# A float32 decoder trunk on one Trainium2 core: the split weights moved by 12 bytes modulo 512, the recurrent section's split operands moved along, the norm's spread written as transposes

## The chip, the core and the metric

The kernel runs on one core of a Trainium2 chip. The metric is the device time of one execution in microseconds. The engines are named as in the profile: PE is TensorE's matmul, PEld its weight load, DVE VectorE, ACT ScalarE, POOL GpSimd, SP the engine that issues most of the DMAs.

## The reference

Two layers over 256 tokens of width 1024 in float32, each a token mixer and a squared-ReLU MLP of width 4096, with RMS norms before each and at the end. Layer 0 mixes with a gated recurrence (RG-LRU), layer 1 with sparse attention.

```python
for i in range(DEPTH):                       # 2 layers
    h = _rmsnorm(x, norm_mix[i])
    if i % N_MIXERS == 0:
        x = x + _rglru_mixer(h, rg_w_in, conv, rg_w_a, rg_w_x, rg_lambda, rg_w_out)
    else:
        x = x + _nsa_mixer(h, nsa_w_in, ..., nsa_w_out)
    h = _rmsnorm(x, norm_ffn[i])
    x = x + _sq_relu_mlp(h, mlp_w_up[i], mlp_w_down[i])    # relu(h @ up)^2 @ down
return _rmsnorm(x, norm_final)

def _rmsnorm(x, g):
    return x * rsqrt(mean(x * x, -1) + 1e-6) * g
```

The inputs are x (1, 256, 1024) and the weights, the output has the shape of x, all in float32.

## The kernel before

Everything is held transposed: a tile `xt` of 128 partitions by 8 chunks by 256 tokens holds x. A linear layer multiplies a piece of weights (128 rows by 128 columns, the stationary operand, loaded by PEld) with 256 tokens of activations (the moving operand). To keep float32's precision with TensorE's faster format (float32r), each operand is split into a high part and the remainder, and one product takes three matmuls (`mm3`): high weights with high activations (line 313), high weights with low activations (314), low weights with high activations (315). This form makes up nearly all the matmuls:

```python
    def mm3(ps, wh, wl, xh, xl, start, stop):
        pe.matmul(ps, wh, xh, start=start, stop=False)
        pe.matmul(ps, wh, xl, start=False, stop=False)
        pe.matmul(ps, wl, xh, start=False, stop=stop)
```

Weights come as pieces of 128 x 1024 floats through five raw buffers (`raw`). ACT (or DVE) rounds a piece into one of seven buffers `whi` (lines 273 and 321), DVE subtracts to get `wlo` (lines 282 and 318). A piece is 8 weight blocks of 128 columns, 512 bytes a partition each, and serves 24 matmuls.

The moving operands are: `hhl`, the normed activations with high and low part, for every input projection and the MLP's up-projection; `uhl`, the MLP's hidden activations, for the down-projection; `xbh` and `xbl`, the split result of the recurrence, for its out-projection; `oh` and `ol` for attention's. The gates of the recurrence multiply unsplit float32 weights `gw` with `xb` (line 656).

A norm sums squares over partitions with matmuls against ones (line 491), takes the root and the reciprocal per token as a column `rcol`, and `spread` (line 494 on) turns that column back into a row on all partitions: a matmul with `rcol` broadcast along 128 columns against the identity (line 496), twice, once for each 128 tokens. It is called once in the recurrent section, once at the start of each MLP, once in the attention section and once for the final norm.

In the recurrent and attention sections a planner with costs and due times orders the instructions; in the MLPs the order is as written. The tile pools place the tiles in the order in which they are asked for. Pool `weights` holds the `whi` and `wlo` tiles one behind the other, then come the statistics, then the section's own tiles; the raw buffers, `hhl` and `uhl` are placed from the other end. So the place of a tile is fixed when the program is built. Start addresses in bytes along a partition, modulo 512:

| tile | before | after the change |
|---|---|---|
| whi, wlo (all blocks) | 32 | 20 |
| hhl, uhl, oh, ol, raw | 480 | 480 |
| xbh, xbl | 352 | 480 |
| xb, r, i, y, t | 352 | 352 |
| gw, a2 | 448 | 64 |
| xp (three) | 352, 384, 416 | 480, 0, 32 |

The rest of the tiles keep their place modulo 512.

Of the kernel before, what the change touches and what calls it, by code (L numbers as in the profile page):

```python
# [12 lines left out]
F32 = mybir.dt.float32  # L13
F32R = mybir.dt.float32r
# [5 lines left out]
P = 128  # L20
S = 256
# [9 lines left out]
NRAW, NSPL = 5, 7  # L31
# [193 lines left out]
def trunk_kernel(ctx: ExitStack, tc: tile.TileContext, x_in, vec_in, const_in, w2_in, wts, out):  # L225
    nc = tc.nc
    ctx.enter_context(tc.manual_schedule())
    pe, dve, act, pool = nc.tensor, nc.vector, nc.scalar, nc.gpsimd
# [5 lines left out]
    wpool = ctx.enter_context(tc.tile_pool(name="weights", bufs=1))  # L234
# [3 lines left out]
    def bank(i):  # L238
        return psum.tile([P, 512], F32, name="bank%d" % i, tag="bank%d" % i)
# [9 lines left out]
    WMAX = 1024  # L249
    LOOK = 6  # L250
    raw_t = [rpool.tile([P, WMAX], F32, name="raw%d" % i) for i in range(NRAW)]
    hi_t = [wpool.tile([P, WMAX], F32R, name="whi%d" % i) for i in range(NSPL)]
    lo_t = [wpool.tile([P, WMAX], F32R, name="wlo%d" % i) for i in range(NSPL)]

    def load(i, parts=1):
        n = piece_cols(*order[i])
# [71 lines left out]
    class Section:  # L328
# [73 lines left out]
        def stats(self, srcs, t):  # L402

            b6 = [("ps", 6)]
            st = self.bank(("stats", t), 6, lambda x: x)
            for j, (x, k) in enumerate(srcs):
                self.add("pe", 0.32, lambda e, j=j, x=x: square_sums(st(), x, j == 0, j == len(srcs) - 1), r=[k], w=b6, t=t)
            self.add("act", 0.15, lambda e: e.activation(rcol, st()[:, :2], AF.Sqrt, bias=epst, scale=1.0 / D), r=b6 + ["tab"],
                     w=["rcol"], t=t)
            self.add("dve", 0.08, lambda e: e.reciprocal(rcol, rcol), w=["rcol"], t=t)  # L410
            self.add("pe", 0.43, lambda e: spread(st()), r=["rcol", "cst"], w=b6, t=t)
            self.add("act", 0.26, lambda e: e.copy(rs, st()[:, S:]), r=b6, w=["rs"], t=t)
# [36 lines left out]
    ident = cst[:, C_ID:C_ID + P]  # L449
# [7 lines left out]
    rcol = spool.tile([P, 2], F32, name="rcol")  # L457
# [35 lines left out]
    def spread(st):  # L493

        for i in range(2):
            pe.matmul(st[:, S + i * P:S + (i + 1) * P], rcol[:, i:i + 1].to_broadcast([P, P]), ident, start=True, stop=True)

    def residual(z, m):
        dve.tensor_tensor(xt[:, m], xt[:, m], z, op=OP.add)  # L499
# [2 lines left out]
    with ExitStack() as ph:  # L502
        rg = ph.enter_context(tc.tile_pool(name="rg", bufs=1))
# [91 lines left out]
        small(lambda e: e.tensor_scalar(sp, sp, 4.0, None, op0=OP.mult), [], ["sp"])  # L595

        xb_b, r_b, i_b, y_b, t_b = (rg.tile([P, 8, S], F32, name=n) for n in ("xb", "r", "i", "y", "t"))
        xbh_b, xbl_b = (rg.tile([P, 8, S], F32R, name=n) for n in ("xbh", "xbl"))
        xb, r_t, i_t, y_t, t_t, xbh, xbl = ([x[:, m] for m in range(8)] for x in (xb_b, r_b, i_b, y_b, t_b, xbh_b, xbl_b))
        pair = lambda x, m: x[:, m // 2 * 2:m // 2 * 2 + 2]  # L600
# [665 lines left out]
    st = bank(6)  # L1266
    mlp(1, to_final, up1, lambda: square_sums(st, acc, True, False))
    square_sums(st, sqs[1], False, True)
    act.activation(rcol, st[:, :2], AF.Sqrt, bias=epst, scale=1.0 / D)
    dve.reciprocal(rcol, rcol)  # L1270
    spread(st)

    for i, (a, n) in enumerate(((0, 1), (1, 1), (2, 2), (4, 2), (6, 1), (7, 1))):
# [113 lines left out]
```

## Time and profile before

| | |
|---|---|
| device time, median of 3 runs | 593.89 us (592.77 to 594.01) |
| span of the profiled execution, first to last instruction | 588.7 us |
| what lies between that span and the median | 5.2 us |
| instructions | 12309 |
| mean granted TensorE clock | 0.996 |
| matmul records / weight loads | 4798 / 4798 |

The profiled execution gives its span alone; its own device time is not listed beside it, so a time worked out on the span is carried to the median by those 5.2 us. Times in the profile's rows are counted from the first instruction. A matmul's record has a start and a modelled end, and the next one starts before that end; how fast PE runs is read from the distance of starts. A group's row gives line, engine, operation, output and inputs by tile names, shapes, count, then busy time, mean ns of one, and idle time ahead of it with what ended it.

In order of time the span holds the recurrent section (to about 93 us), the first MLP (to about 270), attention (to about 410) and the second MLP with the final norm.

### The profile page before, as it was taken

What the parts mean: (1) busy time and instruction counts of PE and PEld (TensorE: products, weight loads), DVE (VectorE), ACT (ScalarE), POOL (GpSimd) and SP (SyncE); (2) the same over time, 40 slices, a digit from 0 to 9 for tenths busy, and PEclk for the clock granted to TensorE, in tenths of its full rate; (3) what the DMA queues carried; (4) which work ended last, traced back from release to release, by engine and by line L of the source; (5) the groups of instructions that cost most, each with busy time, mean ns of one, the idle gap of its engine ahead of it and who ended that gap; (6) DMA issues with size and microseconds to landing.
All of it is one profiled execution on the core that took longest, in us unless ns stands there. A gap on an engine that the chain in (4) does not pass through costs nothing.

```text
span 588.7 us, 12309 instructions
## 1 busy us (share of the span) xinstructions
PE 572.6 (97%) x4798; PEld 559.1 (95%) x4798; DVE 421.5 (72%) x862; ACT 356.5 (61%) x711; POOL 75.2 (13%) x110
## 2 busy tenths in 40 slices
PE   7999999999999999999999999989999999999994
PEld 7999999999999999999989997879999999999994
DVE  6899997776766546547679999989876776464522
ACT  7699583766664325336367999996866564343410
POOL 2210000000001113125211532000000000132320
PEclk9999999999999999999999999999999999999998
DMA  8934665665666665657954641143776667466302
GB/s 285 386 119 136 208 221 183 216 206 183 192 201 197 210 205 175 210 188 228 232 197 144 180 128 52 37 125 99 238 201 199 188 206 239 158 183 228 126 2 72
DMA packets 32682, 105.74 MB, mean 180 GB/s; under 512 B 4832, under 2 KB 6496, under 8 KB 32624
## 3 DMA queue, kind: packets, MB, share of 16 engines
q1 hardware_dynamic: 30224, 100.70, 53.3%
q0 software_dynamic: 1824, 3.72, 2.5%
q8 instruction: 38, 0.62, 0.5%
q10 hardware_dynamic: 576, 0.53, 0.3%
q14 instruction: 20, 0.16, 0.1%
HBM read 99.23 MB, written 1.05 MB: 170 GB/s over the span
## 4 chain that ended last, share of the span: by engine, by line
PE 81%; ACT 8%; DVE 6%; issue 3%; DMA 1%; POOL 0%; SPq 0%; DVEq 0%; ACTq 0%; POOLq 0%
PE bank L315 25%; PE bank L313 25%; PE bank L314 25%; PE bank L656 2%; ACT pt L1105 2%; ACT pt L1124 2%; DVE wlo L318 1%; ACT pth L1138 1%; ACT whi L321 1%; PE bank L906 1%; DMA raw<-in_dram 1%; ACT osum L1171 1%; DVE ptl L1139 1%; DVE pt L1102 1%; DVE osum L1174 1%
## 5 line engine op out<-in xcount | busy, mean ns | idle before, releaser
L313 PE MATMUL bank<-hhl,whi 128*128 128x256 f32 x768 | 214.3, 279 | 1.6 <-DVE whi L321 1.6
L315 PE MATMUL bank<-hhl,wlo 128*128 128x256 f32 x768 | 212.7, 277 | 0.8 <-DVE wlo L318 0.8
L314 PE MATMUL bank<-hhl,whi 128*128 128x256 f32 x768 | 212.3, 276 | 0.0
L282 DVE TENSOR_TENSOR wlo<-raw,whi 128x1024 fp32r<-128x1024 f32 x118 | 147.3, 1269 | 2.7 <-ACT whi L273 2.7
L313 PEld LDWEIGHTS bank<-hhl,whi 128*128 128x128 f32 x768 | 144.2, 188 | 2.2 <-ACT whi L321 1.5
L315 PEld LDWEIGHTS bank<-hhl,wlo 128*128 128x128 f32 x768 | 144.2, 188 | 1.6 <-DVE wlo L318 1.4
L314 PEld LDWEIGHTS bank<-hhl,whi 128*128 128x128 f32 x768 | 144.4, 188 | 0.1
L313 PE MATMUL bank<-uhl,whi 128*128 128x256 f32 x512 | 141.4, 276 | 0.0
L315 PE MATMUL bank<-uhl,wlo 128*128 128x256 f32 x512 | 141.4, 276 | 0.0
L314 PE MATMUL bank<-uhl,whi 128*128 128x256 f32 x512 | 141.4, 276 | 0.0
L273 ACT CAST whi<-raw 128x1024 fp32r<-128x1024 f32 x119 | 120.9, 1039 | 23.7 <-issue 18.8
L314 PEld LDWEIGHTS bank<-uhl,whi 128*128 128x128 f32 x512 | 96.1, 188 | 0.0
L313 PEld LDWEIGHTS bank<-uhl,whi 128*128 128x128 f32 x512 | 96.1, 188 | 0.0
L315 PEld LDWEIGHTS bank<-uhl,wlo 128*128 128x128 f32 x512 | 96.1, 188 | 0.0
L318 DVE TENSOR_TENSOR wlo<-raw,whi 128x1024 fp32r<-128x1024 f32 (+3 forms) x72 | 76.0, 1073 | 2.6 <-ACT whi L321 2.6
L499 DVE TENSOR_TENSOR xt<-xt,bank 128x256 f32<-128x256 f32 x40 | 16.0, 417 | 85.6 <-PE bank L315 85.4
L321 ACT CAST whi<-raw 128x1024 fp32r<-128x1024 f32 (+2 forms) x65 | 61.5, 957 | 17.4 <-PE bank L314 9.5
L751 ACT ACTIVATE u<-t 128x256 f32<-128x256 f32 x64 | 26.7, 417 | 54.9 <-DVE t L746 54.9
L746 DVE SCALAR_TENSOR_TENSOR t<-bank,rstd 128x256 f32<-128x256 f32 x64 | 26.9, 423 | 42.5 <-PE bank L315 41.7
L469 POOL TENSOR_TENSOR acc<-xt 128x256 f32<-128x256 f32 x2 | 3.0, 1522 | 301.1 <-DVE xt L499 301.1
L1264 ACT ACTIVATE xg<-xt,vec 128x256 f32<-128x256 f32 x8 | 4.1, 510 | 48.0 <-DVE xt L499 48.0
L1105 ACT ACTIVATE pt<-pt,mx 128x256 f32<-128x256 f32 (+1 forms) x64 | 28.7, 452 | 3.4 <-DVE mx L1102 3.2
(201 smaller groups left out, 830.5 us busy)
## 6 DMA issues: line engine op xcount, KB each, us to landing
raw<-in_dram SPq DMA_DIRECT2D x175, 512.0 KB, 4.3
gw<-in_dram SPq DMA_DIRECT2D x4, 512.0 KB, 8.4
raw<-in_dram SPq DMA_DIRECT2D x6, 256.0 KB, 5.3
xt<-in_dram SPq DMA_DIRECT2D x4, 256.0 KB, 5.0
kh<-th POOLq DMA_DIRECT2D x16, 64.0 KB, 4.2
raw<-in_dram SPq DMA_DIRECT2D x2, 456.0 KB, 4.8
zwoh<-in_dram SPq DMA_DIRECT2D x1, 512.0 KB, 4.9
zwol<-in_dram SPq DMA_DIRECT2D x1, 512.0 KB, 6.2
```

Source lines behind the costliest of these rows:

```text
L273: (act.copy if eng is None else eng.tensor_copy)(hi_t[i % NSPL][:, :n], raw_t[i % NRAW][:, :n])
L282: (eng or dve).tensor_tensor(lo[:, :n], raw_t[i % NRAW][:, :n], hi[:, :n].bitcast(F32), op=OP.subtract)
L313: pe.matmul(ps, wh, xh, start=start, stop=False)
L314: pe.matmul(ps, wh, xl, start=False, stop=False)
L315: pe.matmul(ps, wl, xh, start=False, stop=stop)
L318: return lambda e: e.tensor_tensor(o, a, h.bitcast(F32), op=OP.subtract)
L321: return lambda e: (e.copy if e is act else e.tensor_copy)(o, a)
L499: dve.tensor_tensor(xt[:, m], xt[:, m], z, op=OP.add)
L656: e.matmul(z(), gw[b][:, o:o + P], xb[2 * b + k], start=k == 0, stop=k == 1)
L746: dve.scalar_tensor_tensor(t, z, 0.0, rs, op0=OP.max, op1=OP.mult)
L751: act.activation(u, t, AF.Square)
L1105: add("act", (0.39, 0.49)[qc], lambda e, row=row, j=j: e.activation(row, row, AF.Exp, bias=mx[:, j:j + 1], scale=-1.0, accum_out=sm[:, j:j ...
```

## The change

The fourteen tiles of split weights become slices of one tile `whl`, each 1024 floats; 120 floats are left free ahead of it and the slices begin 5 floats into it. So all weights lie 12 bytes lower modulo 512, and what follows them in memory lies 512 bytes higher, the same modulo 512. In the recurrent section 32 floats are left free ahead of `xbh` and `xbl`, which moves these two and what follows them (`xp`, `a2`, `gw`) by 128 bytes: `xbh` and `xbl` stand at the same distance from the weights as `hhl` does. The two matmuls of `spread` become transposes (a matmul with the transpose flag) of the same operands. Every engine executes the same instructions in the same order with the same waits.

```diff
     raw_t = [rpool.tile([P, WMAX], F32, name="raw%d" % i) for i in range(NRAW)]
-    hi_t = [wpool.tile([P, WMAX], F32R, name="whi%d" % i) for i in range(NSPL)]
-    lo_t = [wpool.tile([P, WMAX], F32R, name="wlo%d" % i) for i in range(NSPL)]
+    wpool.tile([P, 120], F32, name="wgap")
+    w_all = wpool.tile([P, 2 * NSPL * WMAX + 8], F32R, name="whl")
+    hi_t, lo_t = ([w_all[:, 5 + (i + j * NSPL) * WMAX:5 + (i + j * NSPL + 1) * WMAX] for i in range(NSPL)] for j in range(2))
 
@@
     def spread(st):
 
         for i in range(2):
-            pe.matmul(st[:, S + i * P:S + (i + 1) * P], rcol[:, i:i + 1].to_broadcast([P, P]), ident, start=True, stop=True)
+            pe.transpose(st[:, S + i * P:S + (i + 1) * P], rcol[:, i:i + 1].to_broadcast([P, P]), ident)
 
@@
         xb_b, r_b, i_b, y_b, t_b = (rg.tile([P, 8, S], F32, name=n) for n in ("xb", "r", "i", "y", "t"))
+        rg.tile([P, 32], F32, name="rgap")
         xbh_b, xbl_b = (rg.tile([P, 8, S], F32R, name=n) for n in ("xbh", "xbl"))
```

## The prediction

> **What bounds the kernel now.** I read the shares of the engines first, then the chain that ended last, then the busy time of the engines in stretches of 20 us, and last the starts of single matmuls. Page, engines' shares and the chain by engine and line:
>
> ```profile
> PE 572.6 (97%) x4798; PEld 559.1 (95%) x4798; DVE 421.5 (72%) x862; ACT 356.5 (61%) x711; POOL 75.2 (13%) x110
> PEclk9999999999999999999999999999999999999998
> PE 81%; ACT 8%; DVE 6%; issue 3%; DMA 1%; POOL 0%; SPq 0%; DVEq 0%; ACTq 0%; POOLq 0%
> ```
>
> TensorE (PE) is the bound: 97% busy, 81% of the chain, at the full granted clock. "Busy" hides how fast it runs, since matmuls overlap. The stretches (each: width, then busy time and instructions of PE, PEld, DVE, ACT, POOL, then clock and DMA) say where nothing else holds it:
>
> ```profile
> 0.00:20.00 20.00, 16.70 (x125) 15.92 (x126) 14.16 (x35) 13.98 (x31) 5.44 (x12) 1.00 0.86 308
> 40.00:60.00 20.00, 20.00 (x160) 19.48 (x159) 20.00 (x32) 19.82 (x33) 0.00 (x0) 1.00 0.42 130
> 140.00:160.00 20.00, 20.00 (x179) 20.00 (x178) 14.12 (x22) 12.62 (x23) 0.00 (x0) 1.00 0.64 201
> 360.00:380.00 20.00, 19.11 (x137) 16.65 (x137) 18.28 (x77) 19.90 (x64) 0.00 (x0) 1.00 0.09 27
> 520.00:540.00 20.00, 20.00 (x179) 20.00 (x178) 9.84 (x9) 7.79 (x10) 6.31 (x4) 1.00 0.61 196
> ```
>
> Outside the first 20 us and the attention stage (300 to 400 us, where ACT at 19.90 of 20 holds PE) matmuls stand back to back, and the time of a stage is their number times their spacing. So the starts decide. Timeline of PE: the first and last of 179 rows in the first MLP's up-projection (moving operand hhl), the first and last of 138 in the recurrent out-projection (xbh, xbl), the first and last of 11 in the last down-projection (uhl), and the first and last of 11 just after a norm's statistics:
>
> ```profile
> 139.80 0.28 PE L313 MATMUL bank<-hhl,whi 128*128 128x256 f32 x1
> ...
> 159.98 0.28 PE L314 MATMUL bank<-hhl,whi 128*128 128x256 f32 x1
> 71.77 0.28 PE L315 MATMUL bank<-xbh,wlo 128*128 128x256 f32 x1
> ...
> 87.91 0.28 PE L314 MATMUL bank<-xbl,whi 128*128 128x256 f32 x1
> 574.74 0.28 PE L314 MATMUL bank<-uhl,whi 128*128 128x256 f32 x1
> ...
> 575.87 0.28 PE L315 MATMUL bank<-uhl,wlo 128*128 128x256 f32 x1
> 93.51 0.28 PE L314 MATMUL bank<-hhl,whi 128*128 128x256 f32 x1
> ...
> 94.69 0.28 PE L315 MATMUL bank<-hhl,wlo 128*128 128x256 f32 x1
> ```
>
> Spacings: hhl 20.18 / 178 = 113.4 ns; xbh 16.14 / 137 = 117.8 ns; uhl 1.13 / 10 = 113 ns; after the statistics 1.18 / 10 = 118 ns. The instruction is the same in all four: 128 weights against 256 columns. By the tiles' addresses the moving operand stands (start modulo 512) 448 bytes above the weights for hhl and uhl (480 against 32), 320 for xbh and xbl (352 against 32). So the spacing depends on where the two operands lie to each other, and at 448 there are two speeds, the slow one after a disturbance.
>
> How low can it go? Four groups bound it: matmuls of 32 columns, where only the weight load takes time (six from 301.92 to 302.59), gate matmuls of 256 columns in two passes, transposes of 128 columns (three in a row, six in a row), and PE's groups that carry the sum:
>
> ```profile
> 301.92 0.37 PE L1032 MATMUL bank<-kc,sb 128*128 128x32 f32 x2
> 302.14 0.37 PE L1032 MATMUL bank<-kc,sa 128*128 128x32 f32 x2
> 302.37 0.37 PE L1032 MATMUL bank<-kc,sb 128*128 128x32 f32 x2
> 302.59 0.39 PE L965 MATMUL bank<-whi,hhl 128*128 128x304 f32 x1
> 32.17 2.54 PE L656 MATMUL bank<-xb,gw 128*128 128x256 f32 x11
> 365.26 0.49 PE L1135 MATMUL bank<-cst,pt 128*128 128x128 f32 x3
> 381.07 0.82 PE L1135 MATMUL bank<-cst,pt 128*128 128x128 f32 x6
> L313 PE MATMUL bank<-hhl,whi 128*128 128x256 f32 x768 | 214.3, 279 | 1.6 <-DVE whi L321 1.6
> L313 PE MATMUL bank<-uhl,whi 128*128 128x256 f32 x512 | 141.4, 276 | 0.0
> L313 PE MATMUL bank<-xbh,whi 128*128 128x256 f32 x64 | 17.9, 279 | 0.0
> L656 PE MATMUL bank<-xb,gw 128*128 128x256 f32 x64 | 14.1, 379 | 0.0
> ```
>
> Weight loads alone: 0.67 us / 6 = 111.7 ns. Gates: (2.54 - 0.379) / 10 = 216 ns a pass, so 108 ns for what 256 columns in one pass would stream. Every matmul here has a load of its own (4798 of each), so I take 111.7 ns as the floor of a pair and 108 as the floor of streaming alone. The kernel is 1.7 ns above the first.
>
> **The change part by part.** The order of instructions and every wait stay; only addresses and one flag move, so no queue is passed and no wait is added. The weights lie at 20 modulo 512 instead of 32; hhl and uhl stay at 480, so the distance goes from 448 to 460; rgap puts xbh and xbl at 480 too.
>
> 1. *hhl and uhl, 3 x 768 + 3 x 512 = 3,840 matmuls.* Less, by their starts, some 50 in the first 20 us and 230 in the attention stage, 3,560 stand where PE is the bound. No row has a distance of 460. Its price lies between the floor (111.7, a gain of 1.7 x 3,560 = 6.1 us; 108 if streaming alone counted, 5.4 x 3,560 = 19.2 us) and the slow spacing of the out-projection (117.8, a loss of 4.4 x 3,560 = 15.7 us). I take the floor. Reason: weights are read while the previous matmul streams (PEld is as full as PE, 20.00 of 20). The gates, whose pass streams its columns at half the rate, so that the two reads keep their distance, pay nothing; one-pass matmuls overtake the weight read once. A load reads 128 weights in about the time of 256 columns, so the stream gains 2 bytes a column, and half of 512 less the distance says at which column it catches up: 96 columns at 320, 32 at 448, 26 at 460. At 96 it costs 6.1 ns over the floor, at 32 only 1.7 ns: nearly over before the load has begun. Six columns earlier the rest should go. That it happens at the start and not at the end of the stream is inferred.
>
> 2. *xbh and xbl, 3 x 64 = 192.* From 117.8 to the spacing of part 1: 6.1 x 192 = 1.2 us at the floor, 4.4 x 192 = 0.8 us if only the distance of 448 were kept. All of it is on the path (PE busy 20.00 in the stretch from 80 us, shown below).
>
> ```profile
> 80.00:100.00 20.00, 20.00 (x175) 20.00 (x174) 16.79 (x29) 11.08 (x20) 0.00 (x0) 1.00 0.51 166
> ```
>
> 3. *Spread by transposes, five times two.* An fp32 matmul is two records; ten are twenty:
>
> ```profile
> 94.80 0.61 PE L496 MATMUL bank<-cst,rcol 128*128 128x128 f32 x4
> 95.17 0.37 PE L313 MATMUL bank<-hhl,whi 128*128 128x256 f32 x1
> 581.62 0.71 PE L496 MATMUL bank<-cst,rcol 128*128 128x128 f32 x4 [0.55 <-DVE rcol L1270]
> ```
>
> The transposes above take one record each, (0.82 - 0.49) / 3 = 110 ns apart, so two of the four records of a spread, 0.37 / 4 = 93 ns each from the first to the next matmul's start, or 110 by the transposes' own row, fall away: 0.2 us in the MLP lead-ins, and 0.25 to 0.33 at the end, where nothing covers it. Sum 4 x 0.2 + 0.3 = 1.1 us; I take 1.0, since the recurrent and attention ones stand near DVE's limit. Bounds 0.3 (the end alone) to 1.3.
>
> 4. *DVE and ACT on the moved weights.*
>
> ```profile
> L282 DVE TENSOR_TENSOR wlo<-raw,whi 128x1024 fp32r<-128x1024 f32 x118 | 147.3, 1269 | 2.7 <-ACT whi L273 2.7
> L273 ACT CAST whi<-raw 128x1024 fp32r<-128x1024 f32 x119 | 120.9, 1039 | 23.7 <-issue 18.8
> L318 DVE TENSOR_TENSOR wlo<-raw,whi 128x1024 fp32r<-128x1024 f32 x57 | 68.6, 1215 | 2.6 <-ACT whi L321 2.6
> ```
>
> Taken as unchanged. The MLP hides them: DVE has 6 us of 20 free where PE is full. If they grew 10% (0.12 us each), only the recurrent section (DVE 20.00 of 20) would show it: 11 splits, 1.3 us. A faster PE asks for a weight piece every 24 x 111.7 = 2.68 us instead of 2.72; DMA at a 0.64 share keeps up.
>
> 5. *Gates.* gw and a2 shift by 128 bytes; the gates' distance goes from 416 to 288. Cost nothing, bounded by the 64 matmuls' 216 ns growing as part 1 grew at worst: 64 x 6 = 0.4 us.
>
> 6. *Runs at 118 ns after the statistics*, about 10 to 17 matmuls each: kept; at most 0.7 us if they vanish.
>
> Sum: 6.1 + 1.2 + 1.0 = 8.3 us. In the profiled execution the span goes from 588.7 to 580.4 us; the median of the runs, 593.9, stands 5.2 above that span, so I expect 585.6 us. A difference of 0.2% (1.2 us) is about what a measurement here can tell from none.
>
> **The rivals.**
>
> *A. Wrong side (slower).* The overtaking at 32 columns is cheap because it happens late against the end of the load, and 26 brings it into the middle. Then all pay 117.8 ns: +15.7 - 1.0 = 608.6 us. For it: at 448 a second state of 118 ns already exists and holds for 11 rows. Against: the cost falls from 96 to 32, and I read on in the same direction. It decides from 113.7 ns up.
>
> *B. An odd start costs (slower).* 20 is no multiple of 16, 32 or 64; each load may touch a piece of memory more. Taken as large as part 1's gain, with the other sign: +6.1 + 0.2 - 1.0, about 598 us, from 114 ns up. Against: no weight load of the trace starts so, and nothing shows such a cost. The same page of the Trainium skill, section "Specifications (TRN2)", gives 16-byte lines with a penalty for each new one, which is this rival; no run here shows it.
>
> *C. Only the distance of the out-projection counts (slightly faster).* 12 bytes are too few; hhl and uhl stay at 113.4: -0.8 - 1.0 = 592.0 us. For it: all distances of one-pass matmuls of 256 columns in the trace are multiples of 64, so nothing is known of a smaller step.
>
> *D. No floor at 111.7 (much faster).* The load is hidden, and pairs run at 109 to 110 ns as the transposes do: -4 x 3,560 - 8 x 192 ns - 1.0 = 577 us. Against: the 32-column rows. The Trainium skill, "TensorE: Matmul & The Clock Gate", section "Back-to-back issue gap", gives 262 cycles (109 ns) for 256 columns, which is this rival.
>
> *E. The distance does not matter.* The 4.4 ns between hhl and xbh come from something else in those stages, and part 3 alone remains: 592.9 us. Against: the two rows are the same instruction, at the same clock, with PE full, and differ only in where the moving operand lies. The Trainium skill, "SBUF — State Buffer", section "Who interferes with whom", would have it so: it says that TensorE has independent read ports for moving operand and weights and that "PE and ACT never wait on anyone". The 113.4 and 117.8 ns disagree with that.
>
> **How the numbers follow.** Forecast 0.52; A 0.11; B 0.08; C 0.15; D 0.12; E 0.02. The time is the forecast's, 585.6 us; its own range, with part 1 between 111.3 and 112.6 ns, is 582 to 590. For 8 in 10 the range reaches from 577 to 595, which leaves out A, B and the lower half of D. Faster: forecast, D and two thirds of C, 0.74; same: the rest of C and E, 0.07; slower: A and B, 0.19.
>
> **What would show it.** Right: hhl, uhl and xbh rows all spaced 111 to 112.5 ns; L496 as ten records; the last L496 group near 0.4 us. Part 1 is wrong if hhl stays at 113.4 (C) or rises (A, B); part 2 if xbh differs from hhl; part 3 if the time from the last reciprocal to the first product stays. What would make it wrong above all: the inferred place of the overtaking, which rests on two distances.

## The result, and the profile after

| | before | after |
|---|---|---|
| device time, median of 22 runs each | 594.09 us (591.40 to 601.15) | 590.91 us (589.73 to 593.63) |
| ratio of the two | | 0.9943, 95% interval 0.9921 to 0.9965 |
| device time and span of the profiled execution | span 588.7 us | 590.70 us, span 588.9 us |

The kernel became 3.2 us faster (0.6%), inside the range, but the likeliest case was 8.3 us. A part of the difference is that before has slower executions which after lacks: six of its 22 runs took 598.1 to 601.2 us, none of after's was above 593.7, and with those six set aside the means are 593.34 and 591.27 us, a ratio of 0.9965.

The page of the profile after: engines' shares, the chain by engine, and the groups that answer to those of before (hhl, uhl, and the split of the weights by DVE and ACT).

```profile
PE 572.6 (97%) x4788; PEld 559.2 (95%) x4788; DVE 421.8 (72%) x862; ACT 357.0 (61%) x711; POOL 75.5 (13%) x110
PE 78%; ACT 8%; DVE 6%; issue 3%; DMA 3%; SPq 1%; POOL 1%; DVEq 0%; ACTq 0%; POOLq 0%
L314 PE MATMUL bank<-hhl,whl 128*128 128x256 f32 x768 | 215.1, 280 | 1.0 <-DVE whl L322 1.0
L314 PE MATMUL bank<-uhl,whl 128*128 128x256 f32 x512 | 141.4, 276 | 0.0
L283 DVE TENSOR_TENSOR whl<-raw,whl 128x1024 fp32r<-128x1024 f32 x118 | 147.5, 1271 | 2.7 <-ACT whl L274 2.7
L274 ACT CAST whl<-raw 128x1024 fp32r<-128x1024 f32 x119 | 121.3, 1042 | 24.2 <-issue 18.8
```

PE has the same 572.6 us of busy time with ten records less (ten matmuls of the spreads are one record now instead of two, and each record had a weight load; otherwise the instructions are the same). uhl's busy time is the same 141.4 us to the tenth. DVE's split takes 1271 ns against 1269, ACT's 1042 against 1039. The stretches of 20 us below (columns as in the prediction: the number in brackets behind the first busy time is the matmuls that touch the stretch) show the pace directly: 179 matmuls are a spacing of 113.3 ns, 172 are 117.8. First three stretches of before (out-projection, first MLP, second MLP), then the same of after:

```profile
70.00:90.00 20.00, 20.00 (x173) 20.00 (x171) 18.36 (x35) 14.86 (x25) 0.00 (x0) 1.00 0.64 213
140.00:160.00 20.00, 20.00 (x179) 20.00 (x178) 14.12 (x22) 12.62 (x23) 0.00 (x0) 1.00 0.64 201
460.00:480.00 20.00, 20.00 (x179) 20.00 (x179) 14.20 (x22) 12.62 (x24) 0.00 (x0) 1.00 0.64 203
```

```profile
70.00:90.00 20.00, 20.00 (x179) 20.00 (x178) 19.05 (x35) 15.64 (x26) 0.00 (x0) 1.00 0.68 225
140.00:160.00 20.00, 20.00 (x179) 20.00 (x178) 13.72 (x22) 12.46 (x22) 0.00 (x0) 1.00 0.60 196
460.00:480.00 20.00, 20.00 (x179) 20.00 (x178) 14.21 (x24) 12.39 (x24) 0.00 (x0) 1.00 0.66 192
```

The out-projection went from 173 to 179; both MLPs stay at 179. Timeline of PE after, first the rows around the first MLP's norm (statistics L492, spread L497), then the end of the kernel:

```profile
92.77 0.50 PE L492 MATMUL bank<-ones,acc 128*128 128x1 f32 x4
93.13 0.36 PE L314 MATMUL bank<-hhl,whl 128*128 128x256 f32 x1
...
94.47 0.28 PE L316 MATMUL bank<-hhl,whl 128*128 128x256 f32 x1
94.59 0.38 PE L497 MATMUL bank<-cst,rcol 128*128 128x128 f32 x2
94.72 0.37 PE L314 MATMUL bank<-hhl,whl 128*128 128x256 f32 x1
...
579.59 0.28 PE L316 MATMUL bank<-uhl,whl 128*128 128x256 f32 x1
580.90 0.61 PE L492 MATMUL bank<-ones,sq 128*128 128x1 f32 x4 [1.04 <-DVE sq L465]
582.06 0.43 PE L497 MATMUL bank<-cst,rcol 128*128 128x128 f32 x2 [0.55 <-DVE rcol L1272]
```

A spread is two records instead of four, and 0.13 us pass from its start to the next product (94.59 to 94.72) instead of 0.37. At the end the group takes 0.43 us instead of 0.71. By the starts of single matmuls the stages of the two traces compare so:

| stage, from start to start | before | after |
|---|---|---|
| up to the first gate matmul | 27.70 | 28.50 |
| gates, to the first out-projection matmul | 38.54 | 38.43 |
| out-projection, to the first MLP's statistics | 26.71 | 25.84 |
| to the first down-projection matmul | 83.92 | 83.68 |
| down-projection | 87.04 | 87.04 |
| attention, three stages | 25.05 + 66.91 + 47.80 | 26.12 + 67.05 + 47.79 |
| second MLP's up-projection | 88.00 | 87.76 |
| its down-projection, to the last uhl | 87.48 | 87.39 |
| norm and end | 9.61 | 9.33 |

The three edits' own places give -0.87 - 0.24 - 0.24 - 0.28 = -1.6 us. The start and the first attention stage are longer in this trace by 0.8 and 1.1 us. Of the 0.8 us, 0.3 us is pace: 75 matmuls of the first input projection, with hhl at 460, ran at (18.79 - 10.08) / 74 = 117.7 ns, where before has 113.3. First and last of them:

```profile
10.08 0.28 PE L314 MATMUL bank<-hhl,whl 128*128 128x256 f32 x1
...
18.79 0.28 PE L316 MATMUL bank<-hhl,whl 128*128 128x256 f32 x1
```

In the second trace of after (experiment 3) the same stretch has 113.3 ns. The rest varies as much between executions of one kernel (below), so that the two spans are equal. The profiled execution of after has 1.8 us between span and device time. With 1.8 us, before's 588.7 us span belongs to an execution of about 590.5 us, faster than any of the 22 runs: what the prediction carried over as 5.2 us was mostly scatter between executions.

### The profile page after: what moved, and what is told of

It reads as the page before. It is cut to its first block, busy times and chain, and to the rows that moved or that the text cites. A ratio compares the mean times of both kernels' runs of the same rounds, so it can differ in the third digit from the quotient of the medians.

```text
span 588.9 us, 12289 instructions
## 1 busy us (share of the span) xinstructions
PE 572.6 (97%) x4788; PEld 559.2 (95%) x4788; DVE 421.8 (72%) x862; ACT 357.0 (61%) x711; POOL 75.5 (13%) x110
## 4 chain that ended last, share of the span: by engine, by line
PE 78%; ACT 8%; DVE 6%; issue 3%; DMA 3%; SPq 1%; POOL 1%; DVEq 0%; ACTq 0%; POOLq 0%
PE bank L314 24%; PE bank L316 24%; PE bank L315 24%; PE bank L658 2%; ACT pt L1107 2%; ACT pt L1126 2%; DMA kl<-tl 2%; DVE whl L319 1%; ACT pth L1140 1%; ACT whl L322 1%; PE bank L908 1%; DMA raw<-in_dram 1%; ACT osum L1173 1%; SPq L347 1%; DVE ptl L1141 1%
## 5 line engine op out<-in xcount | busy, mean ns | idle before, releaser
L314 PE MATMUL bank<-hhl,whl 128*128 128x256 f32 x768 | 215.1, 280 | 1.0 <-DVE whl L322 1.0
L316 PE MATMUL bank<-hhl,whl 128*128 128x256 f32 x768 | 213.5, 278 | 0.8 <-DVE whl L319 0.8
L315 PE MATMUL bank<-hhl,whl 128*128 128x256 f32 x768 | 213.0, 277 | 0.0
L283 DVE TENSOR_TENSOR whl<-raw,whl 128x1024 fp32r<-128x1024 f32 x118 | 147.5, 1271 | 2.7 <-ACT whl L274 2.7
L314 PEld LDWEIGHTS bank<-hhl,whl 128*128 128x128 f32 x768 | 145.0, 189 | 1.5 <-ACT whl L322 1.2
L316 PEld LDWEIGHTS bank<-hhl,whl 128*128 128x128 f32 x768 | 144.8, 189 | 1.4 <-DVE whl L319 1.4
L315 PEld LDWEIGHTS bank<-hhl,whl 128*128 128x128 f32 x768 | 145.0, 189 | 0.1
L314 PE MATMUL bank<-uhl,whl 128*128 128x256 f32 x512 | 141.4, 276 | 0.0
L316 PE MATMUL bank<-uhl,whl 128*128 128x256 f32 x512 | 141.3, 276 | 0.0
L315 PE MATMUL bank<-uhl,whl 128*128 128x256 f32 x512 | 141.3, 276 | 0.0
L274 ACT CAST whl<-raw 128x1024 fp32r<-128x1024 f32 x119 | 121.3, 1042 | 24.2 <-issue 18.8
L314 PEld LDWEIGHTS bank<-uhl,whl 128*128 128x128 f32 x512 | 96.1, 188 | 0.0
L315 PEld LDWEIGHTS bank<-uhl,whl 128*128 128x128 f32 x512 | 96.1, 188 | 0.0
L316 PEld LDWEIGHTS bank<-uhl,whl 128*128 128x128 f32 x512 | 96.1, 188 | 0.0
L319 DVE TENSOR_TENSOR whl<-raw,whl 128x1024 fp32r<-128x1024 f32 (+3 forms) x72 | 76.4, 1078 | 2.6 <-ACT whl L322 1.4
L322 ACT CAST whl<-raw 128x1024 fp32r<-128x1024 f32 (+2 forms) x65 | 61.4, 957 | 18.2 <-PE bank L315 10.4
```

Source lines behind the costliest of these rows:

```text
L274: (act.copy if eng is None else eng.tensor_copy)(hi_t[i % NSPL][:, :n], raw_t[i % NRAW][:, :n])
L283: (eng or dve).tensor_tensor(lo[:, :n], raw_t[i % NRAW][:, :n], hi[:, :n].bitcast(F32), op=OP.subtract)
L319: return lambda e: e.tensor_tensor(o, a, h.bitcast(F32), op=OP.subtract)
L322: return lambda e: (e.copy if e is act else e.tensor_copy)(o, a)
```

## The experiments

All kernels are the kernel before with the edit shown. "Pace" is the mean distance of starts of matmuls of 256 columns.

**1. The 12 bytes alone.**

```diff
-    hi_t = [wpool.tile([P, WMAX], F32R, name="whi%d" % i) for i in range(NSPL)]
-    lo_t = ...
+    wpool.tile([P, 120], F32, name="wgap")
+    w_all = wpool.tile([P, 2 * NSPL * WMAX + 8], F32R, name="whl")
+    hi_t, lo_t = ...   # as in the change; no rgap, spread by matmuls
```

> The weights at 20 modulo 512, the rest as before (xbh and xbl then at a distance of 332, the spread as matmuls). Theory 1: 113.3 ns is the floor of a locked pace of load and stream, so the steady spacing of hhl and uhl stays at 113.3 ns; what the 12 bytes change is that after a disturbance (statistics, spread, gates) the 118 ns pace falls back to 113.3 within 10 matmuls instead of lasting to the next disturbance, and that the executions of the kernel before that lie at 594 us and above are those in which the 118 ns pace held for a long stretch. Then: runs between 590.5 and 594 us with none above 595, median some 1.5 us under the kernel before, ratio about 0.9975; xbh still near 118 ns. Theory 2 (the 12 bytes do nothing; the gain of the whole change is the out-projection's 0.87 us and the spread's 1.2 us): ratio 1.000, and the same scatter as the kernel before, up to 600 us.

Measured: 592.52 us (12 runs), ratio 0.9999 (0.9984 to 1.0014). The first two of the three stretches:

```profile
70.00:90.00 20.00, 20.00 (x171) 20.00 (x171) 18.26 (x34) 15.01 (x25) 0.00 (x0) 1.00 0.65 214
140.00:160.00 20.00, 20.00 (x179) 20.00 (x178) 14.22 (x23) 12.66 (x24) 0.00 (x0) 1.00 0.61 201
```

The MLP's pace is 113.3 ns at distance 460 as at 448, and the out-projection, now at distance 332, has 118.2 ns. The term of 6.1 us is not there. The ratio is the second theory's; that no run is above 595.0 is the first's.

**2. The rest without the 12 bytes** (rgap and the transposes).

```diff
+        rg.tile([P, 32], F32, name="rgap")
-            pe.matmul(st[:, ...], rcol[:, i:i + 1].to_broadcast([P, P]), ident, start=True, stop=True)
+            pe.transpose(st[:, ...], rcol[:, i:i + 1].to_broadcast([P, P]), ident)
```

> The change without its shift: weights at 32 as before, rgap (xbh and xbl at a distance of 448) and the transposes kept. Theory 1: xbh may run at 113.3 ns but can also stay at 118 where it starts disturbed; the slow executions of the kernel before remain (some runs above 596 us), median 1 to 2 us under it, ratio about 0.997, and slower than the whole change. Theory 2: xbh at 113.3 ns, ratio 0.9945 as the whole change has it.

Measured: 598.41 us (6 runs), ratio 1.0093 (1.0058 to 1.0128): slower, which neither theory had, so the parts do not add up. The three stretches:

```profile
70.00:90.00 20.00, 20.00 (x172) 20.00 (x171) 18.60 (x34) 15.27 (x26) 0.00 (x0) 1.00 0.69 219
140.00:160.00 20.00, 20.00 (x179) 20.00 (x178) 14.21 (x24) 12.30 (x23) 0.00 (x0) 1.00 0.61 197
460.00:480.00 20.00, 20.00 (x172) 20.00 (x171) 13.38 (x22) 11.69 (x21) 0.00 (x0) 1.00 0.61 186
```

At distance 448 the out-projection has the 117.8 ns that it had at 320, and the second MLP, whose operands did not move, runs at 117.8 ns in 1,445 matmuls in a row: 1,445 x 4.44 = 6.4 us.

**3. The two kernels again, on one chip.**

> The kernel before once more, for its scatter and another trace. Both: ratio 1.000 within 0.2%. Theory 1: the times fall in groups near 592, 594 and 598 to 601 us, and a profile taken in one of the upper groups shows runs of hundreds of matmuls at 118 ns, 4.4 ns each, that add up to its distance from 592 (600 matmuls for 2.7 us). Theory 2: every trace shows the same 118 ns runs of 10 to 20 matmuls, and an upper group's extra time lies in waits for DMA or in the attention stage.

> The changed kernel once more beside the others. Both: ratio 0.992 to 0.9965. Theory 1: no run of more than 80 matmuls at 118 ns or slower in the trace, times within 589.5 to 594 us. Theory 2: the same scatter as the kernel before, 2 us lower.

Measured: before against itself 1.0008 (0.9996 to 1.0021), after 591.33 us, 0.9979 (0.9961 to 0.9997). In the second trace of before the stages up to the gates, and the first two of attention, are longer than in the first one by 0.8, 1.9 and 1.2 us, with MLPs alike: this is the scatter met above. No trace fell on one of before's executions near 600 us. The ratio of after lies above the range that both theories gave. Its second trace also has what the first theory excluded: 103 matmuls at 120.0 ns in a row, from the end of attention (397.8 us) to the statistics of the second MLP, whose up-projection stage takes 88.15 us there instead of 87.76.

**4. Three scans of the distance.** Each of the seven split buffers stands at a place of its own, so consecutive pieces of weights, 24 matmuls each, have different distances to hhl and uhl.

```diff
+    WOFF = (512, 520, 528, 532, 536, 540, 544)
+    w_all = wpool.tile([P, 2 * NSPL * WMAX + 128], F32R, name="whl")
+    hi_t, lo_t = ([w_all[:, (2 * i + j) * WMAX + WOFF[i] // 4 - 8:(2 * i + j + 1) * WMAX + WOFF[i] // 4 - 8]
+                   for i in range(NSPL)] for j in range(2))
+        rg.tile([P, 32], F32, name="rgap")
```

> Each of the seven weight buffers at an offset of its own modulo 512: 0, 8, 16, 20, 24, 28, 32, so distances of 480, 472, 464, 460, 456, 452, 448 follow each other every 24 matmuls, with rgap for xbh. One trace gives a spacing for each. Theory 1 (two paces: 113.3 ns when load and stream are locked, 118 to 120 when not, and no distance goes under 113.3): every distance shows 113 to 114 ns as its fastest steady pace, some fall back to it within 10 matmuls, others keep 118 to 120. Theory 2 (a read conflict that the distance shifts gradually, as the prediction had it): the pace changes with the distance, with values between 111.7 and 118 ns and a best one below 113.

> The same with distances of 440, 432, 416, 384, 0, 496 and 488. Theory 1: again only 113.3 and 117.8 to 120 ns, the distances far from 448 to 460 (384, 0) always at the slow pace. Theory 2: a gradual curve, with its lowest point somewhere between 464 and 0.

> As the other two scans: rgap, and each of the seven split buffers at a place of its own, so that consecutive weight pieces stand at distances 508, 500, 492, 484, 476, 468 and 444 from the moving operand at 480. What is read is the mean spacing of the last 9 of the 24 matmuls of a piece. Theory P (only some distances lock to 113.3 ns, and which ones is not a matter of more or less): most of the seven stand between 117 and 122 ns, at most two at 113.3. Theory D (a falling cost, as the forecast had it): the spacing falls with the distance and reaches 112 ns or less above 480. The total time is 600 to 612 us under P, since pieces at 117 to 120 ns make up most of it, and below 590 under D.

Measured: 606.54, 611.71 and 609.48 us. Pace over the last 9 of a piece's 24 matmuls, median of 18 to 20 pieces:

| distance | 0 | 384 | 416 | 432 | 440 | 444 | **448** | 452 | 456 | **460** | 464 |
|---|---|---|---|---|---|---|---|---|---|---|---|
| ns | 120.0 | 118.8 | 118.7 | 118.8 | 118.8 | 118.3 | **113.3** | 120.0 | 117.4 | **113.3** | 118.2 |

| distance | 468 | 472 | 476 | 480 | 484 | 488 | 492 | 496 | 500 | 508 |
|---|---|---|---|---|---|---|---|---|---|---|
| ns | 118.4 | 119.2 | 120.0 | 118.4 | 116.8 | 121.4 | 119.9 | 118.1 | 116.2 | 118.3 |

Timeline of PE in the first scan: first and last matmul of a piece at 448; then the first, twelfth and last of one at 460, and the first and last of one at 452.

```profile
139.57 0.28 PE L315 MATMUL bank<-hhl,whl 128*128 128x256 f32 x1
...
142.18 0.28 PE L317 MATMUL bank<-hhl,whl 128*128 128x256 f32 x1
```

```profile
131.10 0.28 PE L315 MATMUL bank<-hhl,whl 128*128 128x256 f32 x1
...
132.40 0.28 PE L317 MATMUL bank<-hhl,whl 128*128 128x256 f32 x1
...
133.76 0.28 PE L317 MATMUL bank<-hhl,whl 128*128 128x256 f32 x1
...
136.70 0.29 PE L315 MATMUL bank<-hhl,whl 128*128 128x256 f32 x1
...
139.46 0.28 PE L317 MATMUL bank<-hhl,whl 128*128 128x256 f32 x1
```

At 448: 2.61 / 23 = 113.5 ns, at that pace from the start. At 460: 1.30 / 11 = 118 ns, then 1.36 / 12 = 113.3. At 452: 2.76 / 23 = 120 ns. So the cost does not fall with the distance; the theories of a gradual curve failed, and so did the first theory's 113 to 114 ns for every distance. Of 21 distances two reach 113.3 ns, 12 bytes apart, and 452 between them is among the slowest. None goes below. Each piece starts at the pace that the piece before it left, so a distance was seen from one start alone; since 448 can hold two paces (experiment 7), the scans do not show that the other distances have only the pace seen here. (The moving operand stayed in place and the weights moved, so the scans do not tell whether the distance or the weights' own address counts; that the out-projection had 118.2 ns at 332 and 113.3 at 460 with the same weights speaks against the weights' address alone.)

**5. The second address taken away.** In the second MLP the up-projection's moving operand is one column, broadcast over 256; in its down-projection the weights are one column, broadcast over 128 (both compute something else).

```diff
+    xs = [x[:, k, :1].to_broadcast([P, S]) if layer else x[:, k] for x in (hh, hl)]
+    ws = [x[:, k * P:k * P + 1].to_broadcast([P, P]) if layer else x[:, w] for x in (wh, wl)]
```

> In the second MLP the up-projection's moving operands are one column broadcast to 256 (every column reads one address) and the down-projection's weights one column broadcast to 128; the result is not the reference's, the instructions are the same in number and shape. Theory 1 (113.3 ns is what a load and a stream take in turn, whatever the addresses): 113.3 ns in both stages. Theory 2 (113.3 holds a conflict of reads): 111.7 ns or less where one of the two reads stays at one address.

Measured: 591.01 us. A stretch in the up-projection and one in the down-projection:

```profile
420.00:440.00 20.00, 20.00 (x181) 20.00 (x181) 15.73 (x26) 14.44 (x28) 0.00 (x0) 1.00 0.76 239
520.00:540.00 20.00, 20.00 (x179) 20.00 (x178) 9.46 (x10) 8.21 (x10) 6.31 (x4) 1.00 0.62 198
```

With one moving column the pace is 111.67 ns, and the stage takes 86.84 us instead of 88.00; with one weight column it is 113.3. So each theory held in one of the two stages. The floor of 111.7 ns that the prediction took from the 32-column rows exists for 256 columns too, but the 1.7 ns above it went when the moving operand stopped walking through memory, and not when the weights did.

**6. rgap alone, and rgap with the tiles behind it left in place.**

```diff
+        rg.tile([P, 32], F32, name="rgap")
         xbh_b, xbl_b = ...
+        rg.tile([P, 96], F32, name="rgap2")   # only in the second kernel
```

> The kernel before with rgap alone: xbh and xbl at a distance of 448, weights at 32, the spread as matmuls. Theory 1 (the steady pace needs a good distance and a good start; the spread as matmuls starts the MLPs at 113.3): the MLPs at 113.3 ns as before, the out-projection at 113.3 if the matmuls ahead of it are, ratio 0.9985, up to 1.000 if it starts at 118; far from the 1.009 of the version with transposes. Theory 2 (rgap or the moved gates are what cost the 1.009): ratio above 1.005.

> Only rgap, and behind xbl 384 bytes more, so that gw, a2 and the xp tiles keep their places modulo 512 as before; xbh and xbl go to 480 (distance 448), gates keep 416. Theory G (in the kernel with rgap alone the gates' moved weights set the pace of 117.8 ns from the gates on): the hhl matmuls behind the gates run as before (113.3 with the slow stretch behind the statistics only), xbh at 113.3, both MLPs at 113.3: 192 x 4.4 ns = 0.85 us less, ratio 0.9985. Theory M (the pace at 448 is set by the order of all disturbances, and the out-projection at 448 instead of 320 is one of them, whatever the gates do): the gates' stage as before, but at least one stage of 400 to 1,500 matmuls behind the out-projection at 117.8 ns, ratio 1.003 to 1.02.

Measured: rgap alone 603.72 us (6 runs), 1.0163 (1.0110 to 1.0217); with gw, a2 and xp at their old place modulo 512, 594.06 us (12 runs). These 12 fall into eight of 590.2 to 594.4 and four of 599.2 to 600.5; the ratio of the eight is 1.0003 (0.9980 to 1.0025). The stretches of rgap alone, then of the second kernel:

```profile
70.00:90.00 20.00, 20.00 (x172) 20.00 (x172) 18.07 (x34) 14.71 (x25) 0.00 (x0) 1.00 0.68 209
140.00:160.00 20.00, 20.00 (x172) 20.00 (x172) 13.47 (x22) 11.88 (x22) 0.00 (x0) 1.00 0.60 187
460.00:480.00 20.00, 20.00 (x172) 20.00 (x171) 13.47 (x22) 11.87 (x22) 0.00 (x0) 1.00 0.61 192
```

```profile
70.00:90.00 20.00, 20.00 (x178) 20.00 (x178) 18.90 (x37) 15.61 (x27) 0.00 (x0) 1.00 0.65 213
140.00:160.00 20.00, 20.00 (x179) 20.00 (x178) 13.38 (x23) 12.03 (x22) 0.00 (x0) 1.00 0.57 188
460.00:480.00 20.00, 20.00 (x179) 20.00 (x178) 14.00 (x22) 12.62 (x23) 0.00 (x0) 1.00 0.64 200
```

The same out-projection at the same distance of 448 runs at 117.8 ns behind moved gates and at 113.3 behind gates left in place. What moved in the first kernel alone is gw, a2 and xp, and of these TensorE reads only gw (gates' distance 288 instead of 416). The hhl matmuls woven in behind the gates stay at 117.8 ns from there through 419 matmuls to the end of the out-projection; in the kernel of experiment 2, where gw moved too, the same 419 do. The prediction had priced the move of gw by the gates' own 216 ns, at 0.4 us at most. The second kernel's trace is as theory G has it, with 25.84 us for the out-projection instead of 26.71; in its times that gain does not show.

**7. The transposes alone.** Diff as the second half of 2.

> Only the norm spread by transposes; weights stay at 32 modulo 512 (distance 448 for hhl and uhl) and xbh, xbl at 320. Theory M (at 448 the paces of 113.3 and 117.8 ns both hold themselves, and the last disturbance ahead of a stage decides; with the transposes left out or replaced, the order of disturbances differs): the statistics leave a pace of 117.8 ns, the matmul spread of before happened to end it, and the transposes do not, so at least one whole MLP (1,500 matmuls x 4.4 ns = 6.6 us) runs at 117.8 ns: ratio 1.009 to 1.022, and the rows behind the spread show 117.8 ns to the end of the MLP. Rival S (the transposes only save their records, and the 117.8 ns in the kernel without the shift came from the moved recurrent tiles): 113.3 ns in both MLPs, a gain of 0.24 + 0.24 + 0.28 and some 0.2 us more, ratio 0.998.

Measured: 604.69 us (6 runs), 1.0212 (1.0182 to 1.0242). First and second MLP:

```profile
140.00:160.00 20.00, 20.00 (x172) 20.00 (x171) 13.47 (x22) 11.87 (x22) 0.00 (x0) 1.00 0.58 186
460.00:480.00 20.00, 20.00 (x172) 20.00 (x172) 13.47 (x22) 11.86 (x22) 0.00 (x0) 1.00 0.61 192
```

Ten transposes for ten matmuls, ten records less, and both MLPs run at 117.8 ns: 1,516 + 1,445 matmuls x 4.44 ns = 13.1 us, less the 0.8 us that the records save, against the 12.0 us measured.

**8. One piece of the spread a transpose, the other a matmul.**

```diff
-            pe.matmul(st[:, ...], rcol..., ident, start=True, stop=True)
+            if i == 0:      # second kernel: i == 1
+                pe.transpose(st[:, ...], rcol..., ident)
+            else:
+                pe.matmul(st[:, ...], rcol..., ident, start=True, stop=True)
```

> Weights at 32 modulo 512 as before; of the two pieces of a spread the first is a transpose (one record) and the second stays a matmul (two records). Theory E (the step from the last record of the spread to the first product, 206 ns with matmuls and 201 ns with transposes, sets the pace at 448): the step is 206 ns again, the rows behind it show 113.3 ns, both MLPs run at 113.3, ratio 0.998 to 1.000. Theory R (it is the number of records between the statistics and the products, or the time that the pause takes): with three records instead of four nothing says that the pace returns to 113.3, and at 117.8 the ratio is 1.010 to 1.022.

> The same, in the other order: the first piece stays a matmul and the second is a transpose. Three records as well. Theory E: the step behind the transpose is 201 ns, and both MLPs run at 117.8 ns, ratio 1.02. Theory R: the same as the kernel with the transpose first, whichever that is.

Measured: transpose first 592.90 us (10 runs), 0.9953 (0.9915 to 0.9991). That ratio is no gain of the edit: eight of before's 19 runs beside it took 597.9 to 601.2 us, six of which the ratio counts, and against the mean of the other eleven it is 1.0002. Matmul first 604.41 us (10 runs), 1.0113 (1.0060 to 1.0165; 1.0165 against the same eleven), its runs in two groups, four of 598.0 to 599.9 and six of 604.1 to 605.6. Both have three records in a spread. First and second MLP of the kernel with the transpose first, then with the matmul first:

```profile
140.00:160.00 20.00, 20.00 (x179) 20.00 (x178) 14.21 (x23) 12.61 (x24) 0.00 (x0) 1.00 0.62 204
460.00:480.00 20.00, 20.00 (x179) 20.00 (x178) 13.80 (x22) 12.50 (x22) 0.00 (x0) 1.00 0.66 198
```

```profile
140.00:160.00 20.00, 20.00 (x172) 20.00 (x171) 13.35 (x22) 11.87 (x22) 0.00 (x0) 1.00 0.59 186
460.00:480.00 20.00, 20.00 (x179) 20.00 (x178) 14.21 (x24) 12.47 (x24) 0.00 (x0) 1.00 0.64 192
```

So it is not the number of records that counts, but which kind comes last. The traces' start times, to the nanosecond, of the two norms that open the MLPs ("pace ahead" is between the statistics and the spread, "step" is from the first product behind the spread to the second):

| kernel (distance 448) | first MLP: pace ahead, step, pace behind | second MLP |
|---|---|---|
| before (matmuls) | 118, 206, 113 | 118, 207, 113 |
| rgap, gw in place (matmuls) | 118, 207, 113 | 118, 207, 113 |
| transpose, then matmul | 118, 205, 113 | 118, 205, 113 |
| transposes alone | 118, 201, 118 | 118, 201, 118 |
| matmul, then transpose | 118, 203, 118 | 113, 207, 113 |
| rgap and transposes | 113, 202, 113 | 118, 201, 118 |
| rgap alone (matmuls) | 113, 201, 118 | 113, 201, 118 |

Arriving at 118, a step of 205 to 207 ns led to 113 every time (six of six), 201 to 203 to 118 (four of four). Arriving at 113 the four cases are mixed. What makes the step 4 ns longer or shorter was not found.

Read by the kind of the last piece, which no theory had named ahead of the runs in this form, the table has no mixed case. Three more MLP norms at 448, two in the second trace of before and one in that of experiment 5, are as the first row (118, 206, 113), which makes 17. A spread that ends in a matmul exchanged the two paces in 11 of 11, and one that ends in a transpose kept the pace that it met in 6 of 6. The statistics exchange them too, in 17 of 18 (the 17 and the second MLP of experiment 5; the exception is the first MLP of the kernel with the matmul first, at 118 on both sides). So in before the two exchanges cancel and the MLP goes on at 113; with the transposes alone one is left and it goes on at 118; and rgap alone, which reaches the statistics of both MLPs at 118, leaves both spreads at 118 again. This is a regularity of the MLP norms and not a cause. In the recurrent norm the spreads that end in a transpose also led from 118 to 113 (three of three traces, with steps of 205 and 206 ns), and in the attention norm, where PE waits 0.5 us behind the second product, a step of 206 ns led to 118 (rgap with gw in place, and experiment 5).

The second kernel's theory of "201, both MLPs" held in one MLP of its trace; the two groups of its times roughly fit one and two MLPs at 117.8 (592.9 + 6.7 and + 13.1 us).

At distance 460, in after, the statistics of the second MLP leave 117, 117, 114, 114 ns and the spread 120, 115, 122, 114, 120, 117, 118, 114, and then it is 113.3 again: the slow pace dies out within about ten matmuls. So it went in all six MLPs of the three traces at 460. Elsewhere in these traces it did not always: the 75 matmuls at 117.7 ns shown with the result, the 103 at 120.0 ns of experiment 3, and 147 at 120.0 ns in attention with the shift alone lasted to the next interruption.

## Why the prediction was right or wrong

*Part 1 (6.1 us): this step failed.* hhl and uhl kept 113.3 ns, which is rival C, given 0.15. The inference from two distances (6.1 ns over the floor at 320, 1.7 at 448, so nothing at 460) took the cost for a falling curve; experiment 4 shows isolated values, and 332 (118.2 ns) and 452 (120.0) are no better than 320 (117.8). The floor was real (experiment 5: 111.67 ns), but no distance tried reached it. The explanation by a stream that overtakes the weight read is not borne out; what sets 113.3, 117.8 and 120.0 stays open. The Trainium skill, "SBUF — State Buffer", section "Who interferes with whom", gives TensorE independent read ports for the two operands, by which the place should not matter; the 113.3 ns at 448 beside 120.0 at 452, in one trace and with only the place of the weights changed, do not fit that. The 16-byte lines with a penalty for each new one, which the prediction takes for rival B, stand in the Trainium skill, "SBUF — State Buffer", section "Specifications (TRN2)"; no cost of the odd start shows, with 113.3 ns at 20 as at 32. The Trainium skill, "TensorE: Matmul & The Clock Gate", section "Back-to-back issue gap", gives the 262 cycles (109 ns) of rival D as the gap of an isolated matmul, and says that in a stream of pairs the load counts too; no pair here reached 109 ns, the lowest pace is 111.67.

*Part 2 (1.2 us, or 0.8 at C):* 0.87 us in the trace, 192 x 4.44 ns = 0.85. Right with C's pace. The premise that the distance rather than the tile counts held at 460; at 448 the out-projection ran at 113.3 ns in one kernel and at 117.8 in two, depending on what ran ahead. So the 117.8 ns at 320, on which the prediction's curve rests, are no clean price of a distance either.

*Part 3 (1.0 us):* 0.24 in each MLP as predicted (0.2), 0.28 at the end (0.25 to 0.33); the rest could not be told from the scatter of the recurrent and attention sections. The row 0.13 instead of 0.37 us shows the saving. But the spread was priced at its records alone, and it also sets the pace of what follows: made alone, the transposes cost 12.0 us.

*Part 4:* right: 1271 against 1269 and 1042 against 1039 ns.

*Part 5 (nothing, at most 0.4 us):* the gates' own time is unchanged in after (38.43 us for the stage against 38.54), but with the weights at 448 rgap cost 1.6% with gw moved, and nothing that shows with gw left in place. The bound looked at the moved instruction and not at its successors.

*Part 6 (kept):* at 460 the stretches at 118 after an MLP's norm became about ten matmuls at 114 to 122. This part, taken as worth nothing, is the one that mattered. I had read the two paces at 448 as "the slow one after a disturbance" that ends by itself. In before it ended because the spread by matmuls ended it. At 448 the slow pace, once left alone, holds for a whole MLP; at 460 it died out behind all six MLP norms, though not everywhere else.

*Sums.* Rival B's own terms give 593.9 + 6.1 + 0.2 - 1.0 = 599.2 us, not 598, and leaving out A, B and half of D leaves a chance of 0.75 for the range, not 8 in 10. The range reaches above the time of before (594.1 us), so it is luck and no merit of part 1 that the time lies inside it. Of the 3.2 us only 1.6 lie at the three edits' places; the rest is before's executions near 600 us, of which it is not shown that the change removed them, and scatter.

So the shift gains nothing alone, and the other two edits lose 0.9% without it; together they gain what parts 2 and 3 say. One thing fits but is not shown: 18 of the 111 executions of before took 597.9 to 602.4 us and none took 595.4 to 597.8, while of 46 executions with the weights at 460 (after twice, and the shift alone) none was above 595.0. The 18 are spread unevenly, from none of 17 to eight of 19 in a comparison, and beside those eight the kernel with the transpose first, at 448, had none in ten. An MLP at 117.8 ns would add 6.7 us, the right size; no trace of such an execution of before was taken. It would explain why the comparison (3.4 us by its ratio) exceeds the 1.6 us of the three edits' places. The rest of the difference between the comparisons, 0.9943 and 0.9979, is of the size of the scatter and is left open. No kernel here was faster than after.

## What to carry to other kernels

When one instruction runs at two speeds in a trace, find out what starts and what ends the slow one before pricing anything; an edit of a few instructions at that place can cost many times what they take (five spreads by transposes: 0.8 us saved where the trace can tell, 12.0 us lost when made alone). Two distances do not make a curve: a scan with a different address in each buffer costs one run and shows whether there is one. And test the parts of a change apart, since here each was zero or a loss alone and the whole a gain.

## What was not expected of the hardware

- Pairs of weight load and 256-column matmul with all operands walking have preferred paces, 113.33, 117.78 and 120.0 ns, and in the scans only 448 and 460 of 21 distances modulo 512 lock to the first; most others cycle through patterns such as 117, 117, 123, 132, 117, 119, 115, 118 ns (at 452).
- At 448 both 113.33 and 117.78 ns hold for over 1,400 matmuls; behind an MLP's norm a spread that ended in a matmul exchanged them (11 of 11) and one that ended in a transpose kept them (6 of 6). Why is open. At 460 the slow one died out in about ten matmuls behind all six MLP norms, though runs of 75 at 117.7 ns and of 147 and 103 at 120.0 ns were seen once each elsewhere (after, the shift alone, and after's second trace).
- With a broadcast moving operand the pace is 111.67 ns; broadcast weights changed nothing (113.33).
